# The low parts of split weights on one engine: a layer of attention and experts in fp32 on one core

## The chip, the cores and the metric

One core of a Trainium2 chip runs the whole layer in one launch. The metric is the device time of the execution in microseconds; before the change it is 1330.33 us, the median of 3 runs (1330.31 to 1330.54).

## The reference

256 latent tokens and 256 context tokens of width 1024 go through one layer. Cut to what matters:

```python
h, hc = modulate(x), modulate(ctx)                     # adaLN: RMS norm, scale and shift from c @ ada_w
q_a, k_a, v_a, qa_b, kva_b, gates = split(h @ w_in)    # the same for the context
o_a = attention(rope(norm(q_a)), [kc_a, k_a], [vc_a, v_a])        # 8 heads of 128, 2 of k and v
o_b = attention(mla_q(qa_b), mla_k(kva_b), mla_v(kva_b))          # 8 heads of 128 + 64
y = (sigmoid(g_a) * (o_a @ w_o_gqa) + sigmoid(g_b) * (o_b @ w_o_mla)) @ w_out
x = x + g1 * y
x = x + g2 * moe(modulate(x))                          # the best 4 of 32 experts for each token
```

Keys and queries are RMS-normed with a gain per channel. Of an expert's weights, w1 is 1024 x 2048 and w2 1024 x 1024, all fp32.

## The kernel before

**Two halves.** The first half, up to the choice of the experts, runs the layer's dense part. The second reads all 32 experts' weights, 12 parts of 1 MB each (`expert_part`, L99 to L106), through a ring of 20 buffers, and computes on 64 gathered tokens of each expert. 14 parts are loaded ahead of time by steps of the first half (`EZ` 2 parts, `EA` 8, `EG` 4), into buffers that attention has released; the other 6 buffers (three named w, y0, y1 and r0) come at its end. Each next part waits for a buffer that an expert has used up.

**Products in split precision.** The dense part multiplies in the format fp32r, and gets back the accuracy of fp32 by splitting each operand into a high part (a copy that is rounded) and a low part (what the rounding took off). `mm3` (L171) issues three matmuls: high by high (L173), high by low (L174), low by high (L175). Activations are split by `split` (L167), the copy on ScalarE and the subtraction on VectorE. Weights are split by `wsplit` (L132): the copy wh on ScalarE (L138) and the subtraction wl (L140) on VectorE for every fourth call and on GpSimd for the others. `wsplit` is called 124 times: 16 times in the first projection (`g1_cols`), 8 times in each of 12 chunks of 512 columns (`chunk`, L487: 2 of q, 4 of the gates, 2 each of the two branches' projections and the output's), 8 times in `mla_q` and 4 in `mla_a`. A chunk loads 4 rows of blocks at a time into one of three w buffers, which is free again after the last wh and wl made from it, and splits two blocks ahead of the product.

**Other work on GpSimd.** The rotary tables (`tables`, L397 to L425), the low part of V (L485), the gain of MLA's queries (L670), and in `mla_a` half of the scaling of the keys by their norms: L712 scales tokens' tiles 0 and 1 on GpSimd, L713 tiles 2 and 3 on VectorE, L714 the rotary part on VectorE. The norms come from a chain of some ten small VectorE instructions, `rsqrt` (L177 to L188).

**The order of the work.** Every piece of the first half is a Python generator, a work, which issues its instructions up to the next `yield` when a step of it is asked for. `PLAN` (L23) is a list of such steps, written out; `x*3` is three steps of x. Before a work's first step all works that it needs are finished (`step`, `finish` and `needs`), so the list is not the whole order: in both lists, for example, heads' scores are finished by the first step that needs them. Each engine, and SP as the queue of all loads, runs what it gets in its order; the compiler settles that order within the steps' neighbourhood, and the trace shows small instructions of different steps side by side.

The names that matter here: T0 and T1 transpose and norm the tokens; r, c, f, h, l, k 0 to 7 are the first projection; `bi` loads the experts' biases (3 loads); `tab` the rotary tables; `end` (`g1_end`) copies the projection's results; `ss` (`low_norms`) makes the norms; `kv` keys and values; q0, q1 and g0 to g3 the chunks of queries and gates; `mp`, p, a, b 0 to 3 prepare MLA's heads; S, P, V 0 to 15 are scores, transposed probabilities and values of the 16 heads; wa, wb, o the branches' and output's chunks; `rest` and `late` the last 12 and 4 units of the adaLN projection, each a load of 1 MB; x reloads the tokens; EZ, EA, EG load experts ahead.

```python
        self.nsplit += 1
        self.nc.scalar.copy(h, src)
        eng = self.nc.vector if self.nsplit % 4 == 0 else self.nc.gpsimd
        eng.tensor_sub(l, src, h.bitcast(F32))
```

Of the kernel before, what the change touches and what calls it, by code (L numbers as in the profile page):

```python
# [6 lines left out]
F32 = mybir.dt.float32  # L7
# [14 lines left out]
NA, NC, NS = 8, 4, 4  # L22
AHEAD = 2  # L23
PLAN = """
T0 bi l0 f1 h0 T0 h1 T0 f0 l1 k0 f2 r1 T1 h2 r0 k1 r2 T0 r3 T0 f3 k2 c2 h3 f4 k3 T0 T1 h4 T1 l4 T0 tab T1*2 r5
f5 f6 l3 k4 r4 r7 EZ c0 k5 c1 h6 l2 f7 k6 l5 end T1 q0 ss kv q0 h7 c3 q0 kv r6 q0 kv q1 kv q0*2 h5 q1*3 l7 q1
g0 q0 q1 q0*2 q1 kv EZ mp q1 q0 T1 g0 q1 q0 c7 k7 c5 g0*2 g1 q1*2 g0*3 g1 c4 g0 mp g0 g1 l6 EZ S0 g1*2 S2 g1*2
P0 kv rest g1 g2*3 mp S4 g2 P1 S2 S0 g2*2 end g3 rest*3 g2 rest g1 rest g3 V3 S1 g2 P2 rest P4 S4 V2 S3 c6 P3
g2 g3*3 S5 g3*2 a0 g3 rest S6 rest S1 a0 S5 rest a0 S6 g3 rest*2 a0 rest*3 P5 a0 rest*3 S3 g2 a0 S7 P6 g3 S7
rest V1 V6 a1 V0 rest a1 P7 b0 rest a1*2 S8 rest*2 a1 b0 rest V8 b1 V7 rest b1 rest a2 P9 b0 V5 b0 a1 b0 a0  # L30
rest a2 a1 V4 a2*2 S10*2 V9 b1 S8 a2 a3 a0 b0 V11 a3*4 rest a1 b2 wa0 S12 a3 a0 S9 P11 a2 wa0*2 a2 wa0 P8 wa0
rest wa0 S12 a2 b1 rest wa0*2 rest b1 b2 a3 b2 a1 rest wa0 rest P10 S9 S11 S13 b3 b2 wa1*3 a2 wa1 P12 a3 S13
wa1*3 S11 b3 V12 P13 b1 wa0 a3 b3 S14 V13 S14 EA S15 wb0 wa1 EA*2 wb0 wa1 wb0*2 EA wb0*2 b2 S15 wa1 wb0*3 b2
P14 EA wb1*2 b3 o0 wb1 EG o0 wb0 wb1 V10 rest*2 wb0 o0 P15 wb1 late wb1 o0 EA o0 wb1 o0*2 wb1 rest o0 EA wb1
o1 wb1 late EG*2 rest late o0 o1 o0*2 o1*5 V14 EG wb1 EG V15 wb0 late o1 o0 o1 late x b3 o1 wb1 late EA*2 o1
b3 late o1 late
"""
SLOTS = ("e0", "e1", "e2", "e3", "m0", "m1", "g0", "g1", "y0", "y1", "z0", "z1")
LATER = ("n0", "n1", "n2", "n3")
# [11 lines left out]
class Layer:  # L51
# [81 lines left out]
    def wsplit(self, src):  # L133

        shape = list(src.shape)
        h, l = self.tile("ws", shape, F32R, "wh", NS), self.tile("ws", shape, F32R, "wl", NS)
        self.nsplit += 1
        self.nc.scalar.copy(h, src)  # L138
        eng = self.nc.vector if self.nsplit % 4 == 0 else self.nc.gpsimd
        eng.tensor_sub(l, src, h.bitcast(F32))  # L140
        return h, l

    def bank(self, tag, shape=(128, 512), dt=F32):
# [539 lines left out]
    def mla_a(self, g):  # L683

        nc = self.nc
        G = self.grp[g]
        u = self.w([128, 512])
        nc.sync.dma_start(u, self.I["wmk"][g])
        kh, kl = self.wsplit(u)
        yield  # L690
        ssq, rs = G.pop("ssq"), self.m([128, 12], "grs")
        v = G["v"] = self.s(("e0", "x", "e1", "e0")[g], [128, 2, 4, 2, 128], F32R)
        kn = G["kn"] = self.h("k4", [128, 4, 2, 128])
        for t in range(4):
            ts = slice(t * 128, (t + 1) * 128)
            b = self.bank("acc")
            self.mm3(b, self.ckT[0][:, ts], self.ckT[1][:, ts], kh, kl, start=True, stop=True)
            bv = b.rearrange("p (h c d) -> p h c d", h=2, c=2)
            nc.scalar.copy(kn[:, t], bv[:, :, 0])
            sv = self.a([128, 2, 128])  # L700
            nc.scalar.activation(sv, kn[:, t], AF.Square)
            nc.vector.tensor_reduce(ssq[:, 4 + 2 * t:6 + 2 * t], sv, AX.X, OP.add)
            nc.scalar.copy(v[:, 0, t], bv[:, :, 1])
            nc.vector.tensor_sub(v[:, 1, t], bv[:, :, 1], v[:, 0, t].bitcast(F32))
            yield
        s4 = ssq[:, 4:12].rearrange("p (t h) -> p t h", h=2)
        nc.vector.tensor_add(s4, s4, self.ssr.unsqueeze(2).broadcast_to([128, 4, 2]))
        self.rsqrt(rs, ssq, 1.0 / 192, 12, "r12")
        nc.vector.tensor_scalar_mul(rs[:, 0:4], rs[:, 0:4], 192.0 ** -0.5)
        rk = rs[:, 4:12].rearrange("p (t h) -> p t h", h=2).unsqueeze(3)  # L710
        kr = self.a([128, 4, 2, 64])
        nc.gpsimd.tensor_mul(kn[:, 0:2], kn[:, 0:2], rk[:, 0:2].broadcast_to([128, 2, 2, 128]))  # L712
        nc.vector.tensor_mul(kn[:, 2:4], kn[:, 2:4], rk[:, 2:4].broadcast_to([128, 2, 2, 128]))  # L713
        nc.vector.tensor_mul(kr, self.rk.unsqueeze(2).broadcast_to([128, 4, 2, 64]), rk.broadcast_to([128, 4, 2, 64]))  # L714
        G.update(kr=kr, rs=rs)
        yield
# [572 lines left out]
```

## Time and profile before

| | |
|---|---|
| median of 3 runs | 1330.33 us (1330.31 to 1330.54) |
| the profiled execution | 1328.88 us |
| its span, first to last instruction | 1327.1 us |
| mean granted TensorE clock | 0.979 |
| TensorE busy (PE) | 1216.7 us, 92% |
| VectorE busy (DVE) | 445.8 us, 34% |
| ScalarE busy (ACT) | 289.1 us, 22% |
| GpSimd busy (POOL) | 158.9 us, 12% |
| read from HBM | 465.23 MB, 351 GB/s over the span |

PE, DVE, ACT and POOL are the names of the engines in the profile; SPq is the queue that issues the loads. A group is a line of the kernel, an engine, an operation and the tiles that it writes and reads; behind the bar come its busy time, the mean of one in ns, the idle time of the engine before it and what ended that. The shares of busy time are means over the whole span, of which the first half is less than a third.

### The profile page before, as it was taken

The numbers are of one execution on the slowest core, as the hardware profiler recorded it, in microseconds if no ns is written. First come the engines' busy times: TensorE is split into PE (matmuls) and PEld (weight loads), VectorE is DVE, ScalarE is ACT, GpSimd is POOL, SyncE is SP. The second block draws the span as 40 slices with busy tenths as digits, with TensorE's granted clock in tenths as the row PEclk, the third lists the DMA queues.
The fourth block names the chain that finished last, engine by engine and source line by source line (L and its number), as shares of the span: only waits on it lengthen the run. The fifth ranks groups of instructions, "written<-read, shape, count | busy, mean of one in ns | idle before, by whom it ended". The sixth has DMA issues, their size and how long they took to land.

```text
span 1327.1 us, 15523 instructions
## 1 busy us (share of the span) xinstructions
PE 1216.7 (92%) x6143; PEld 593.4 (45%) x6143; DVE 445.8 (34%) x940; ACT 289.1 (22%) x624; POOL 158.9 (12%) x181
## 2 busy tenths in 40 slices
PE   5989999799989989999999999999898998989896
PEld 4767766578752434333344333433333233333332
DVE  4468467875331332121221212212111122212112
ACT  2366667765420100000010000100000010000000
POOL 1566322343400000000000000000000000000000
PEclk8999999999989999999999999999999999999999
DMA  9825554147869999999999999999999999999995
GB/s 341 320 74 180 189 200 146 64 162 302 348 261 421 420 400 401 421 419 420 419 420 420 420 419 419 420 419 420 420 420 419 420 419 420 420 419 421 419 420 206
DMA packets 67325, 467.34 MB, mean 352 GB/s; under 512 B 7633, under 2 KB 8017, under 8 KB 11953
## 3 DMA queue, kind: packets, MB, share of 16 engines
q1 hardware_dynamic: 67248, 466.30, 86.7%
q8 instruction: 50, 0.82, 0.2%
q14 instruction: 27, 0.21, 0.0%
HBM read 465.23 MB, written 1.05 MB: 351 GB/s over the span
## 4 chain that ended last, share of the span: by engine, by line
PE 52%; DMA 34%; DVE 7%; ACT 2%; issue 2%; POOL 1%; SPq 0%; DVEq 0%; ACTq 0%; POOLq 0%
PE bs L1021 17%; PE bx L1055 10%; DMA r<-in_w_dram 8%; DMA m<-in_w_dram 8%; DMA n<-in_w_dram 7%; DMA w<-in_w_dram 6%; DMA e<-in_w_dram 4%; PE bacc L173 3%; PE bacc L174 3%; PE bacc L175 3%; PE bacc L989 2%; PE bx L191 2%; PE bt L989 2%; PE bacc L1070 1%; PE bs L1014 1%
## 5 line engine op out<-in xcount | busy, mean ns | idle before, releaser
L1030 ACT ACTIVATE a<-a 128x512 f32<-128x512 f32 x32 | 20.1, 630 | 728.9 <-DVE a L1029 728.9
L1029 DVE TENSOR_SCALAR a<-bs 128x512 f32<-128x512 f32 x32 | 22.1, 692 | 436.4 <-PE bs L1021 436.4
L140 POOL TENSOR_TENSOR wl<-w,wh 128x512 fp32r<-128x512 f32 (+1 forms) x81 | 105.8, 1318 | 145.6 <-ACT wh L138 128.7
L999 POOL TENSOR_TENSOR c<-c,gm 128x128 f32<-128x128 f32 x32 | 12.1, 399 | 867.8 <-DVE c L982 850.5
L1061 DVE TENSOR_TENSOR y<-bx,g 64x512 f32<-64x512 f32 x64 | 44.1, 688 | 211.7 <-PE bx L1055 211.0
L1021 PE MATMUL bs<-e,xg 128*64 128x512 f32 x416 | 94.2, 595 | 3.4 <-DMA e<-in_w_dram 3.4
L1021 PE MATMUL bs<-n,xg 128*64 128x512 f32 x400 | 90.8, 595 | 3.6 <-DMA n<-in_w_dram 3.5
L1021 PE MATMUL bs<-w,xg 128*64 128x512 f32 x312 | 72.2, 597 | 5.0 <-DMA w<-in_w_dram 5.0
L989 PE MATMUL bacc<-c,xn 128*128 128x128 f32 x256 | 40.8, 325 | 38.5 <-DVE c L982 37.8
L138 ACT CAST wh<-w 128x512 fp32r<-128x512 f32 (+1 forms) x108 | 65.0, 612 | 46.3 <-PE bacc L175 31.5
L989 PEld LDWEIGHTS bacc<-c,xn 128*128 128x128 f32 x256 | 37.3, 231 | 51.8 <-DVE c L982 51.0
L1021 PEld LDWEIGHTS bs<-e,xg 128*64 128x64 f32 x416 | 28.8, 137 | 66.5 <-issue 55.9
L1021 PEld LDWEIGHTS bs<-n,xg 128*64 128x64 f32 x400 | 27.7, 137 | 64.4 <-issue 56.5
L1021 PE MATMUL bs<-g,xg 128*64 128x512 f32 x208 | 47.7, 598 | 2.2 <-DMA g<-in_w_dram 2.2
L1021 PE MATMUL bs<-y,xg 128*64 128x512 f32 x208 | 47.4, 594 | 2.4 <-DMA y<-in_w_dram 2.4
L1055 PE MATMUL bx<-n,a 128*64 128x512 f32 x208 | 48.9, 614 | 0.7 <-ACT a L1043 0.7
L1021 PE MATMUL bs<-z,xg 128*64 128x512 f32 x208 | 47.5, 596 | 1.1 <-DMA z<-in_w_dram 1.1
L1055 PE MATMUL bx<-e,a 128*64 128x512 f32 x208 | 47.1, 595 | 0.0
L1021 PE MATMUL bs<-m,xg 128*64 128x512 f32 x192 | 44.2, 595 | 2.3 <-DMA m<-in_w_dram 2.3
L1021 PEld LDWEIGHTS bs<-w,xg 128*64 128x64 f32 x312 | 21.1, 136 | 54.0 <-issue 40.5
L989 PE MATMUL bt<-c,xn 128*128 128x128 f32 x256 | 37.3, 294 | 0.0
L989 PEld LDWEIGHTS bt<-c,xn 128*128 128x128 f32 x256 | 35.1, 212 | 0.0
(362 smaller groups left out, 2001.9 us busy)
## 6 DMA issues: line engine op xcount, KB each, us to landing
e<-in_w_dram SPq DMA_DIRECT2D x78, 1024.0 KB, 19.9
n<-in_w_dram SPq DMA_DIRECT2D x76, 1024.0 KB, 19.9
w<-in_w_dram SPq DMA_DIRECT2D x57, 1024.0 KB, 19.9
z<-in_w_dram SPq DMA_DIRECT2D x40, 1024.0 KB, 19.9
m<-in_w_dram SPq DMA_DIRECT2D x38, 1024.0 KB, 19.9
g<-in_w_dram SPq DMA_DIRECT2D x38, 1024.0 KB, 19.9
y<-in_w_dram SPq DMA_DIRECT2D x38, 1024.0 KB, 19.9
w<-in_ada_dram SPq DMA_DIRECT2D x24, 1024.0 KB, 6.5
```

The lines of the kernel that those rows point to most:

```text
L138: self.nc.scalar.copy(h, src)
L140: eng.tensor_sub(l, src, h.bitcast(F32))
L173: mm(o, lh, rh, start=start, stop=False, **kw)
L174: mm(o, lh, rl, start=False, stop=False, **kw)
L175: mm(o, ll, rh, start=False, stop=stop, **kw)
L191: self.nc.tensor.transpose(o, i, self.ident)
L989: nc.tensor.matmul(b[:, kk % 2], self.xn[:, t, kk * 128:(kk + 1) * 128], oh[:, t], start=t == 0, stop=t == 1)
L1021: mm(b[64 * j:64 * j + 64], xg[:, k, e % 2], w[:, lo:lo + 512], start=False, stop=k == 7, tile_position=(0, 64 * j))
L1029: v.tensor_scalar_min(g, gl, 7.0)
L1030: nc.scalar.activation(s, g, AF.Sigmoid, scale=1.702)
L1055: nc.tensor.matmul(b[64 * j:64 * j + 64], lh, w[:, i, j * 512:(j + 1) * 512], start=f == 0, stop=f == 7, tile_position=(0, 64 * j))
L1061: nc.vector.tensor_mul(y[r:r + 64, cs], b[q], self.g2[q, cs])
```

## The change

All 124 low parts of split weights are made on VectorE, and L712's half of the key scaling too, so that one engine makes L712 and L713 one after the other. `PLAN` is another list with the same works.

```diff
@@ PLAN @@
-T0 bi l0 f1 h0 T0 h1 T0 f0 l1 k0 f2 r1 T1 h2 r0 k1 r2 T0 r3 T0 f3 k2 c2 h3 f4 k3 T0 T1 h4 T1 l4 T0 tab T1*2 r5
-f5 f6 l3 k4 r4 r7 EZ c0 k5 c1 h6 l2 f7 k6 l5 end T1 q0 ss kv q0 h7 c3 q0 kv r6 q0 kv q1 kv q0*2 h5 q1*3 l7 q1
-g0 q0 q1 q0*2 q1 kv EZ mp q1 q0 T1 g0 q1 q0 c7 k7 c5 g0*2 g1 q1*2 g0*3 g1 c4 g0 mp g0 g1 l6 EZ S0 g1*2 S2 g1*2
-P0 kv rest g1 g2*3 mp S4 g2 P1 S2 S0 g2*2 end g3 rest*3 g2 rest g1 rest g3 V3 S1 g2 P2 rest P4 S4 V2 S3 c6 P3
-g2 g3*3 S5 g3*2 a0 g3 rest S6 rest S1 a0 S5 rest a0 S6 g3 rest*2 a0 rest*3 P5 a0 rest*3 S3 g2 a0 S7 P6 g3 S7
-rest V1 V6 a1 V0 rest a1 P7 b0 rest a1*2 S8 rest*2 a1 b0 rest V8 b1 V7 rest b1 rest a2 P9 b0 V5 b0 a1 b0 a0
-rest a2 a1 V4 a2*2 S10*2 V9 b1 S8 a2 a3 a0 b0 V11 a3*4 rest a1 b2 wa0 S12 a3 a0 S9 P11 a2 wa0*2 a2 wa0 P8 wa0
-rest wa0 S12 a2 b1 rest wa0*2 rest b1 b2 a3 b2 a1 rest wa0 rest P10 S9 S11 S13 b3 b2 wa1*3 a2 wa1 P12 a3 S13
-wa1*3 S11 b3 V12 P13 b1 wa0 a3 b3 S14 V13 S14 EA S15 wb0 wa1 EA*2 wb0 wa1 wb0*2 EA wb0*2 b2 S15 wa1 wb0*3 b2
-P14 EA wb1*2 b3 o0 wb1 EG o0 wb0 wb1 V10 rest*2 wb0 o0 P15 wb1 late wb1 o0 EA o0 wb1 o0*2 wb1 rest o0 EA wb1
-o1 wb1 late EG*2 rest late o0 o1 o0*2 o1*5 V14 EG wb1 EG V15 wb0 late o1 o0 o1 late x b3 o1 wb1 late EA*2 o1
-b3 late o1 late
+f0 h0 f1 T0 bi T0 h1 T0 l0 l1 k0 f2 r1 T1 k1 r2 r0 c2 r3 T0*2 f3 k2 h3 f4 k3 T0 T1*2 h4 T1 T0 tab T1 r5 f5 f6
+l3 h2 l4 k4 r4 r7 c0 EZ k5 c1 f7 k6 l2 h6 end T1 q0*4 q1 kv*2 ss q0 kv r6 q0 q1 kv q1*2 h5 l7 q1 q0 q1*2 g0 q0
+kv q0 EZ mp rest*2 q1*2 q0 T1 g0 q0 g0 c7 g0 g1 c5 g0 c3 q1 g1 q1 g0*3 mp g1*2 g2 kv h7 S0 g2 EZ l6 P0 g0 g1*2
+rest g2 g1*2 S2 mp P1 g2*3 g3 rest g2 g3 rest g1 rest S1 c4 S2 P2 l5 end g2 S0 rest S4 S6 rest V3 V2 S4 S3 P3
+g3 rest g3*2 S5 S3 c6 g3*2 g2 P4 a0 g3 rest*2 a0 S6 g3 a0 rest a0*2 P5 rest*2 S5 rest V1 rest g2 S7 P6 rest*3
+g3 S7 V6 a1 rest b0 k7 rest V0 a1*3 P7 S8 rest*2 a1 rest a0 V8 rest b1 V7 b1 b0 S1 b0 rest a2 P9 b0 V5 a0*2
+rest a2 a1 a2*2 a1 b0 S10*2 V9 V4 a2 a3 b1 rest wa0 b0 b2 S8 V11 a3*4 a1 P13 a1 wa0 a3 a2*2 wa0 S12 rest*2 wa0
+S12 rest b1 wa0 P8 wa0 b1 rest wa0 b2 P12 S11 S13 wa0 wa1 rest S9 S15 a3 P10 b2 wa1 wa0 a2 wa1 S9 a2 a3 S13
+wa1*3 b3 a0 wa1 S11 b3 V12 V13 b2 S14*2 EA a3 wa1 wb0 b3 EA wb0 b2 P11 wb0 EA S15 wa1 wb0*3 rest wb0 EA wa1
+wa0 wb1 b3 wb0*2 wb1 P14 b2 EA wb1 o0 late o0 wb1 rest wb1 o0 P15 wb1 late wb1 EA o0 wb1 o0*2 b1 o0 EA wb1
+o1*2 wb1 late o0 o1*2 o0 EG*2 o1 o0*2 rest o1 V14 EG*2 V15 wb0 wb1 late wb0 o0 wb0 o1 late x EG V10 rest o1 b3
+o1 EA wb1 late*3 EA b3 o1*3
@@ wsplit @@
-        eng = self.nc.vector if self.nsplit % 4 == 0 else self.nc.gpsimd
-        eng.tensor_sub(l, src, h.bitcast(F32))
+        self.nc.vector.tensor_sub(l, src, h.bitcast(F32))
@@ mla_a @@
-        nc.gpsimd.tensor_mul(kn[:, 0:2], kn[:, 0:2], rk[:, 0:2].broadcast_to([128, 2, 2, 128]))
+        nc.vector.tensor_mul(kn[:, 0:2], kn[:, 0:2], rk[:, 0:2].broadcast_to([128, 2, 2, 128]))
```

With what each first step finishes written out, the lists differ in these places. `r0`, `c0` come ahead of T0, and T1 ahead of the second unit of the projection; `bi` comes behind that unit. The second half of `end`, and `ss`, came after one step of q0 and now come after four of q0 and one of q1. Two steps of `rest` stand in the midst of q1. wa0 begins ahead of the last scores of heads 10 and 11 and not behind their values, and the scores of 12 and 13 stand together ahead of most of wa0. EA's last three loads and EG's first, which came right behind o0's first step, now stand behind its third, seventh and ninth; EG's other three move by a step or two. `late` begins behind o0's first step and ends ahead of o1's last three, where its last step was the last of all.

## Rows read from the trace of the kernel before

**Rows 1.** Busy time by stage (a:b, us, then PE, PEld, DVE, ACT, POOL, PEclk, DMA, GB/s).

```profile
30.00:70.00 40.00, 39.69 (x275) 30.32 (x274) 20.43 (x44) 14.01 (x32) 18.97 (x35) 1.00 0.80 307
70.00:98.00 28.00, 22.91 (x95) 17.46 (x94) 17.46 (x32) 18.66 (x53) 19.36 (x21) 0.94 0.21 75
98.00:190.00 92.00, 89.45 (x507) 68.81 (x509) 57.67 (x136) 63.74 (x127) 39.46 (x31) 1.00 0.49 169
190.00:270.00 80.00, 68.18 (x450) 49.11 (x442) 66.07 (x180) 56.37 (x135) 19.13 (x18) 0.96 0.36 129
270.00:376.00 106.00, 105.16 (x578) 81.11 (x576) 54.07 (x106) 54.91 (x111) 45.42 (x34) 1.00 0.72 276
376.00:390.00 14.00, 9.79 (x60) 8.07 (x61) 8.25 (x39) 5.86 (x12) 0.76 (x2) 0.76 0.78 317
390.00:1327.10 937.10, 865.74 (x4106) 326.54 (x4104) 208.47 (x359) 67.63 (x141) 11.35 (x30) 0.98 0.99 409
```

**Rows 2.** The same view, two microseconds at the first expert.

```profile
390.00:392.00 2.00, 2.00 (x10) 0.62 (x10) 0.00 (x0) 0.16 (x1) 0.00 (x0) 1.00 0.00 0
```

**Rows 3.** Timeline of SP, the issue of loads, 376 to 393 us.

```profile
376.80 0.74 SPq L105 DMA_DIRECT2D r<-in_w_dram  x1
391.83 0.33 SPq L105 DMA_DIRECT2D z<-in_w_dram  x1
```

**Rows 4.** The chain that ended last, 0 to 390 us, by line.

```profile
by line: PE bacc L173 9.1%; PE bacc L174 8.7%; PE bacc L175 8.5%; issue 4.3%; PE bx L278 4.3%; DMA w<-in_ada_dram 3.6%; PE bt L191 3.2%; POOL wl L140 2.6%; PE bx L191 2.5%; PE bt L174 2.2%; PE bt L175 2.1%; PE bt L173 2.0%; PE bs L173 2.0%;
```

**Rows 5.** Line 140, the low parts: ns min/median/max, first and last start; who waited.

```profile
L140 POOL TENSOR_TENSOR wl<-w,wh x81: 1012/1303/1759, 70.8 to 365.6; 128x512 fp32r<-128x512 f32 x75, 128x384 fp32r<-128x384 f32 x6
...
L140 DVE TENSOR_TENSOR wl<-w,wh x27: 548/693/2007, 78.0 to 366.3; 128x512 fp32r<-128x512 f32 x25, 128x384 fp32r<-128x384 f32 x2
...
  PE bt L174: 3.4, 4
```

**Rows 6.** Timeline of POOL and of DVE, 83 to 89 us (start, us).

```profile
83.41 4.22 POOL L140 TENSOR_TENSOR wl<-w,wh 128x512 fp32r<-128x512 f32 x3
...
83.92 1.23 DVE L182 TENSOR_SCALAR r_v<-kssq 128x14 f32<-128x14 f32 x1
86.44 1.23 DVE L186 TENSOR_TENSOR r_t<-krstd 128x14 f32<-128x14 f32 x1
88.11 0.17 DVE L186 TENSOR_TENSOR r_t<-krstd 128x14 f32<-128x14 f32 x1
```

**Rows 7.** Timeline of POOL and of SP, 44 to 52 us.

```profile
44.59 0.21 POOL L405 COPY rb<-h 128x32 f32<-128x32 f32 x1 [5.36 <-DMA h<-in_rows_dram]
50.04 1.29 POOL L140 TENSOR_TENSOR wl<-h,wh 128x512 fp32r<-128x512 f32 x1
...
51.36 0.33 SPq L321 DMA_DIRECT2D h<-in_wg_dram  x1
```

**Rows 8.** Busy time by stretch, around the first rsqrt chain.

```profile
84.00:94.00 10.00, 5.22 (x19) 3.38 (x20) 8.54 (x19) 4.45 (x13) 5.82 (x6) 1.00 0.00 0
94.00:97.40 3.40, 3.40 (x10) 2.66 (x9) 1.53 (x4) 1.80 (x5) 3.00 (x6) 0.52 0.83 308
```

**Rows 9.** Line 140 alone by stage: DVE busy, POOL busy, PEclk, DMA, GB/s.

```profile
98.00:190.00 92.00, 8.13 (x9) 37.87 (x29) 1.00 0.49 169
190.00:270.00 80.00, 2.52 (x3) 10.51 (x9) 0.96 0.36 129
270.00:376.00 106.00, 10.62 (x12) 43.91 (x33) 1.00 0.72 276
```

**Rows 10.** Groups of instructions, 190 to 270 us: the scaling of MLA's keys.

```profile
L713 DVE TENSOR_TENSOR k<-k,grs 128x512 f32<-128x512 f32 x3 | 4.0, 1333 | 0.0
L712 POOL TENSOR_TENSOR k<-k,grs 128x512 f32<-128x512 f32 x3 | 3.6, 1209 | 18.0 <-DVE grs L188 18.0
L714 DVE TENSOR_TENSOR a<-rk,grs 128x512 f32<-128x512 f32 x3 | 3.2, 1051 | 0.0
```

**Rows 11.** PE's waits, 0 to 390 us (in total, times, longest).

```profile
PE bx L278 <- DMA w<-in_ada_dram: 3.6, 3, 1.4
```

## The prediction

> **What bounds the kernel now.** The span of the core is 1327.1 us. The profiled execution took 1328.88 us, 1.45 below the median of the three runs, 1330.33; the sum below is made against the first and carried to the second by the same difference. I cut the span into stages [rows 1]. From 390 us on the DMA engines are busy 99% of the time and move 409 GB/s: the experts' weights arrive no faster than that, and 409 GB/s over 937.1 us is 383 MB, the 364 parts of 1.049 MB that are still to come (384 less the 20 that lie in SBUF by then) and the output. The change touches nothing there.
>
> What starts this stream is the first expert matmul. Between 390 and 392 us the DMA engines stand still [rows 2]: the last of the 20 buffers was issued at 376.80, and the next load, at 391.83, could only be issued when the first expert had used up z0 [rows 3]. So the time is the moment at which the experts begin, plus a constant: a microsecond won or lost before 390 us is won or lost at the end, as long as the 20 parts are there in time. For that there is room: 28% of 270 to 376 and 22% of 376 to 390 us, 30 + 3 = 33 us of idle DMA [rows 1].
>
> Ahead of 390 us the reader is to look at what PE lacks in each stage [rows 1]: 0.3 us of 40 in 30 to 70, 5.1 of 28 in 70 to 98, 2.6 of 92 in 98 to 190, 11.8 of 80 in 190 to 270, 0.8 of 106 after it. A gain has to come out of these, or out of time at the lower clock. The chain of waits up to 390 us is mostly PE; POOL's low parts hold 2.6% of it, 10.1 us [rows 4].
>
> **What the change removes.** Of the 124 low parts every fourth is made on VectorE now, so 93 are POOL's, at a median of 1.30 us; VectorE takes 0.69 [rows 5]. PE waited 3.4 us, in 4 cases, for POOL's low parts on their largest line [rows 5], and the view names no wait for one of VectorE's. Two more things are less plain:
> - POOL holds VectorE up. While POOL made three low parts in a row from 83.41 on, an r_v and an r_t of 14 elements took 1.23 us each on VectorE; with POOL done, at 88.11, the same line took 0.17 [rows 6]. A VectorE low part takes 2.0 us at most where the median is 0.69 [rows 5]: one POOL low part fits into the difference. This goes with POOL's instructions. The Trainium skill ("SBUF — State Buffer", "Who interferes with whom") calls it an exclusive lock of the port pair that the two engines share, for a whole instruction; the trace agrees, 2.0 being 0.69 + 1.30. By it the 1.23 fall to 0.17; without it they would stay, and 2 of the 5 us that I take below at 84 us would drop out.
> - POOL's low parts stand in a queue with its other work. The rotary tables began at 44.59, after POOL had waited 5.36 us for a load, and low parts stood between them; the weight load of 51.36 waited for the one that began at 50.04 [rows 7].
>
> **Stage by stage, the terms of the sum.**
> - 30 to 70 us: the low parts leave the queue behind the tables, so that load can go up to 5 us earlier. PE lacks only 0.3 us here [rows 1]. Between 0 and 5, I take 1, near PE's row. The three loads of `biases`, now behind the second pair of weight loads, are needed by no one before the experts: nothing.
> - 70 to 98 us: PE works 5.22 us of the 10 from 84 on, waiting for POOL's low parts and for ScalarE, which waited for the rsqrt chain that POOL had stretched; then it runs 3.4 us at 0.52 of its clock, the 1.2 GHz level, which costs 0.48 of them, 1.6 us [rows 8]. The change takes both causes away and, beside that, puts the second half of `g1_end` and `low_norms` behind three more steps of q0 and the first of q1, so that PE has those products to do meanwhile. What these two issue on ACT and DVE moves past the copies and low parts of that stretch, and the load of q1's first unit goes ahead of it on SP. Between 0 and 6.4, I take 5. The low part of V (L485) stays on POOL and can still hold VectorE up once.
> - 98 to 190 us: 29 low parts move [rows 9]. If they were late as often as POOL's were in that row (4 of 93) by one instruction of VectorE, this would cost 29 × 4 / 93 × 0.69 = 0.9; the most to be had is PE's 2.6. I take 1.
> - 190 to 270 us, the MLA heads: VectorE is busy 66 of 80 us and POOL makes 9 low parts and 3 key scalings there [rows 1, 9, 10]. Twelve instructions more at 0.69 are 8.3 us. Against that, L713 takes 1333 ns and L714 1051 where 690 would do, 3 × (0.64 + 0.36) = 3.0 us, and the same holds for the small instructions that I can't count. The key scaling itself: L712 takes 1209 ns beside L713's 1333; after the change the two follow each other, 2 × 0.69 = 1.38, so that pair costs nothing. The bounds are a loss of 8.3, all twelve in the way, and a gain of 11.8, all that PE lacks. I take a gain of 2, close to the middle: VectorE's own load hardly grows, and each low part is there 0.6 us sooner.
> - 270 to 376 us: 33 low parts [rows 9], PE lacks 0.8 [rows 1]; as above a loss of 33 × 4 / 93 × 0.69 = 1.0 or a gain of 0.8. I take 0.5.
> - The moved steps. Of `rest`, two steps go ahead of most of g0 and the others are spread more evenly; each unit is a load of 1 MB, its products and a copy or an addition. PE waited 3.6 us in all for these loads [rows 11], so 3.6 either way; I take 0. `late` (4 such loads) now begins right behind o0's first step and ends before o1's last three, on the same PE, with the same work: 0. wa0's first load and splits go ahead of the last of heads 10 and 11, five low parts' time (3.5 us) at most, in a stretch counted above. EA's last three expert loads and EG's first go behind up to eight steps of o0, on SP's queue past the loads of wout and `late`. This would cost only beyond the 33 us of idle DMA above, so nothing; with that cover gone each part is 2.6 us (1.049 MB at 409 GB/s).
>
> The sum: 1 + 5 + 1 + 2 + 0.5 = 9.5 us less, 1319.4 in a profiled execution and **1320.8** as a median.
>
> **Rivals.**
> - VectorE becomes the bound in the MLA stretch (slower). In-order, a low part now stands behind a reduction that waits for scores, and a rsqrt chain behind low parts. Price: the 8.3 in full, 0.9 and 1.0 in the neighbouring stages, less the 5 at 84 us, which doesn't hang on it: 5.2 later, 1335.5. For it: 66 of 80 us busy already. Against it: part of those 66 are POOL's doing. It decides from some 74 of the 80 us on (66 + 8.3, no relief).
> - Nothing that can be told (within 0.2%, 2.7 us, which is about what a measurement of this kernel can tell from no change). PE waited just 3.4 us for low parts; where they come sooner, the next wait takes over, a load of the ada weights or ScalarE's copies, which stand ahead of every low part and don't change. It would give 1329. The Trainium skill ("Perfetto Trace Analysis", "Optimizing Scalar/DVE Operations") warns that offloading between VectorE and GpSimd might not help, because they share a read port; by that rule the time stays where it is. The rows speak half against it: port time falls from 1.30 to 0.69 per low part.
> - Far more: the chain's 10.1 us of POOL halve, the stretch from 84 us closes (6.4), and half of what PE lacks from 190 to 270 us goes (6): 17 us, 1313. Against it: VectorE's 8.3 us have to go somewhere.
>
> **How the numbers follow.** The forecast, 3 to 14 us faster, has 0.58; far more, 0.12; no change, 0.12; VectorE as the bound, 0.18. So faster 0.70, same 0.12, slower 0.18. The range leaves out the far half of the last case and the far half of "far more": 1311 to 1335. Its upper end is also about the sum of the lower bounds (0 + 0 - 0.9 - 8.3 - 1.0, with the 5 at 84 us). The likeliest case's own range is 1316 to 1328.
>
> **What would show it.** Right: the experts begin near 380 us, with the DMA engines idle just before; PE is busy over 8 of the 10 us around the first rsqrt chain, and the clock doesn't fall there; r_t never takes over 0.3 us from then on save beside V's split; L713 near 0.69. VectorE's low parts: 124 at a median near 0.69. Wrong: PE waits for VectorE's low parts for more than the 3.4 us that it now waits for POOL's; VectorE busy over 74 of the 80 us of the MLA stretch; PE's idle time there above 11.8; or no idle DMA before the first expert load that follows a free buffer, which would mean that the 20 parts came late.

## The result and the profile after

The changed kernel takes **1318.58 us** (median of 4 runs, 1318.11 to 1319.53), the kernel before 1330.42 beside it (4 runs, 1330.31 to 1330.54): a ratio of 0.9912, with an interval of 0.9895 to 0.9929, 11.8 us less. The prediction was 1320.8 us, faster. Lines behind the edit in the function that splits weights are one lower than before: its low part is L139 now, the key scaling L711 to L713.

The profiled execution took 1318.76 us, its span is 1317.0. From the page, the busy time of the engines:

```profile
PE 1220.3 (93%) x6143; PEld 594.7 (45%) x6143; DVE 475.4 (36%) x1037; ACT 289.3 (22%) x624; POOL 36.8 (3%) x84
```

GpSimd lost 122 us of work and VectorE won 30. Busy time by stage comes next (a:b, us, then PE, PEld, DVE, ACT, POOL, PEclk, DMA, GB/s); the stages are those of [rows 1], the bounds at 376 and 390 us moved to where the same work ends now and the others kept, so that the work between them is not quite the same, and behind them the first rsqrt chain, the two microseconds behind the first expert matmul, and all that lies ahead of it:

```profile
30.00:70.00 40.00, 40.00 (x275) 30.79 (x274) 20.39 (x51) 14.41 (x32) 9.38 (x26) 1.00 0.77 301
70.00:98.00 28.00, 26.13 (x130) 20.25 (x129) 22.92 (x49) 23.17 (x62) 7.36 (x11) 1.00 0.41 151
98.00:190.00 92.00, 91.02 (x534) 67.39 (x534) 69.48 (x177) 62.60 (x128) 1.67 (x2) 1.00 0.50 182
190.00:270.00 80.00, 73.80 (x434) 54.29 (x434) 70.63 (x209) 61.66 (x147) 5.31 (x6) 0.98 0.35 127
270.00:362.70 92.70, 90.94 (x499) 70.84 (x497) 58.50 (x104) 44.73 (x87) 0.00 (x0) 1.00 0.73 277
362.70:376.70 14.00, 10.69 (x74) 8.24 (x74) 7.92 (x38) 4.93 (x12) 0.76 (x2) 0.76 0.90 345
376.70:1317.00 940.30, 868.89 (x4110) 329.05 (x4106) 208.69 (x359) 68.83 (x141) 11.39 (x30) 0.98 0.99 408
78.00:88.00 10.00, 9.24 (x39) 6.96 (x38) 9.24 (x24) 8.13 (x28) 2.19 (x2) 1.00 0.30 116
...
376.70:378.70 2.00, 2.00 (x14) 0.77 (x12) 0.00 (x0) 0.00 (x0) 0.00 (x0) 1.00 0.01 4
0.00:376.70 376.70, 351.37 (x2038) 265.66 (x2038) 266.69 (x678) 220.47 (x483) 25.45 (x54) 0.97 0.60 223
```

The same view of the kernel before, up to its first expert matmul:

```profile
0.00:389.85 389.85, 350.80 (x2038) 266.71 (x2038) 237.29 (x581) 221.35 (x484) 147.55 (x151) 0.97 0.58 215
```

Read the two last rows against each other. PE does the same 2038 matmuls in the same 351 us, but in a span 13.15 us shorter: all of the gain is time that PE stood idle (39.05 us before, 25.33 after). VectorE has 97 instructions more (93 low parts and 4 scalings). At the 0.60 us from one to the next that the timeline below shows, they would add 58 us. They add 29.4. The other 29 us are time by which VectorE's other instructions had been longer: those that the edit doesn't touch, group by group the same number in both traces, take 24.7 us less in sum, and the low parts that were VectorE's already another 6.

That shows in line 139 itself (ns min/median/max, first and last start), the row that answers to [rows 5]:

```profile
L139 DVE TENSOR_TENSOR wl<-w,wh x108: 537/692/2467, 68.9 to 352.7; 128x512 fp32r<-128x512 f32 x100, 128x384 fp32r<-128x384 f32 x8
```

and in the timeline of VectorE around the first rsqrt chain, which answers to [rows 6]:

```profile
77.84 3.67 DVE L139 TENSOR_TENSOR wl<-w,wh 128x512 fp32r<-128x512 f32 x3 [0.37 <-ACT wh L138]
81.44 0.16 DVE L181 TENSOR_SCALAR r_v<-kssq 128x14 f32<-128x14 f32 x1
...
81.84 0.17 DVE L185 TENSOR_TENSOR r_t<-krstd 128x14 f32<-128x14 f32 x1
...
83.45 0.68 DVE L139 TENSOR_TENSOR wl<-w,wh 128x512 fp32r<-128x512 f32 x1
84.05 0.16 DVE L185 TENSOR_TENSOR r_t<-krstd 128x14 f32<-128x14 f32 x1
```

r_v and r_t take 0.16 and 0.17 us, where they took 1.23 each. The median of the low parts stayed (693 to 692 ns), but one of them takes 2.47 us: it is one of the three from 77.84 on (3.67 together), and the timeline of GpSimd says beside what it ran:

```profile
77.37 2.39 POOL L484 TENSOR_TENSOR m<-y,m 128x1024 fp32r<-128x1024 f32 x1 [1.54 <-ACT m L483]
```

That is the low part of V, the one large subtraction which stayed on GpSimd.

In the stretch from 190 to 270 us the key scaling, as groups (busy us, mean ns), for [rows 10]:

```profile
L711 DVE TENSOR_TENSOR k<-k,grs 128x512 f32<-128x512 f32 x4 | 2.7, 684 | 0.0
L712 DVE TENSOR_TENSOR k<-k,grs 128x512 f32<-128x512 f32 x4 | 2.7, 680 | 0.0
L713 DVE TENSOR_TENSOR a<-rk,grs 128x512 f32<-128x512 f32 x3 | 2.0, 682 | 0.0
```

PE's waits up to 376.7 us (in total, times, longest), for [rows 5, 11]:

```profile
PE bx L277 <- DMA w<-in_ada_dram: 2.5, 2, 1.4
...
PE bt L173 <- DVE wl L139: 0.8, 1, 0.8
```

and the queue of loads at the start of the experts, for [rows 3]:

```profile
366.27 0.44 SPq L105 DMA_DIRECT2D r<-in_w_dram  x1
378.68 0.33 SPq L105 DMA_DIRECT2D z<-in_w_dram  x1
```

**Where the time went.** Following the same piece of work in both timelines: the copy that ends the first projection starts 1.3 us earlier (74.76 to 73.48), the first scaling of a key behind the rsqrt 4.7 (89.37 to 84.67), the last tanh of the gates 6.7 (181.20 to 174.52), the last scaling of MLA's keys (the half that moved) 11.9 (279.33 to 267.45), the last step of the output's second chunk 13.7 (373.17 to 359.44), and the first expert matmul 13.15 (389.85 to 376.70). But the span is only 10.1 us shorter: 3.05 us are given back behind the first expert matmul (937.25 us to the end before, 940.30 after). These are single executions. In a second trace of the new kernel the first expert matmul is at 378.03 and the end 940.57 behind it. The kernel before has one trace, and one of a kernel that differs from it only behind this matmul has the first scaling of a key at 91.25 and the last tanh at 183.37, some 2 us later. So a stage's gain is known to a microsecond or two.

### The profile page after: what moved, and what is told of

The parts are those of the page before. It is cut to its first block, busy times and chain, and to the rows that moved or that the text cites. A ratio compares the mean times of both kernels' runs of the same rounds, so it can differ in the third digit from the quotient of the medians.

```text
span 1317.0 us, 15464 instructions
## 1 busy us (share of the span) xinstructions
PE 1220.3 (93%) x6143; PEld 594.7 (45%) x6143; DVE 475.4 (36%) x1037; ACT 289.3 (22%) x624; POOL 36.8 (3%) x84
## 4 chain that ended last, share of the span: by engine, by line
PE 65%; DMA 27%; DVE 5%; ACT 2%; issue 1%; SPq 0%; POOL 0%; DVEq 0%; ACTq 0%; POOLq 0%
PE bs L1020 21%; PE bx L1054 11%; DMA r<-in_w_dram 8%; DMA m<-in_w_dram 6%; DMA n<-in_w_dram 5%; DMA e<-in_w_dram 5%; PE bacc L172 3%; PE bacc L173 3%; PE bacc L174 3%; DMA w<-in_w_dram 3%; PE bacc L988 2%; PE bx L277 2%; PE bx L190 2%; PE bacc L1069 2%; PE bt L988 2%; PE bt L1069 2%
## 5 line engine op out<-in xcount | busy, mean ns | idle before, releaser
L139 DVE TENSOR_TENSOR wl<-w,wh 128x512 fp32r<-128x512 f32 (+1 forms) x108 | 74.6, 696 | 30.1 <-ACT wh L138 29.4
```

The lines of the kernel that those rows point to most:

```text
L139: self.nc.vector.tensor_sub(l, src, h.bitcast(F32))
```

## The experiments

The theory: GpSimd's low parts read SBUF, and while they do, VectorE's instructions stand still; taking them away frees VectorE, whose results PE waits for. A first rival says that the new order of the work does it, and the engines nothing. A second says that it is GpSimd's queue, and that a low part is simply there 0.6 us sooner. A question of its own is where the 3 us went.

### The engines and the order apart

One kernel has the new engines in the order of before, the other the old engines in the new order: `PLAN` of one file stands in the other.

> Only the engines change: all low parts and the key scaling on VectorE, the list of steps is that of before. Theory A (the gain comes from POOL's work leaving: shorter low parts, and VectorE no longer held up): at least two thirds of the 11.8 us, so 1318 to 1322.5 us. Rival B (the gain comes from the new order): 1326 or more. Rival C (VectorE in the old order is in the way, and the new list was needed to avoid that): 1331 or more.

> Only the list of steps changes, three of four low parts and half of the key scaling stay on POOL. Theory A: a gain of at most 4 us, 1326 to 1331. Rival B: 1322 or less. If the two parts add up, this one's gain is 11.8 less that of the engines alone; if they don't, each needs the other.

Measured: the engines alone 1322.36 us (9 runs), a ratio of 0.9944 (0.9928 to 0.9961); the order alone 1330.6 us (10 runs), 1.0006 (0.9989 to 1.0023). So the engines give 7.4 us, a little under the two thirds of 11.8 that theory A asked for (7.9), though inside its range of times; the order by itself gives nothing that can be told, and the two together 11.8: the order is worth some 4 us once the engines are changed (the intervals of 0.9944 and 0.9912 just touch), and only then. In the profiles the first expert matmul is at 382.17 and 388.53, against 376.70 with both. The first r_v takes 0.16 us with the engines alone and 1.27 with the order alone: what held it up goes with the engines. The first scaling of a key starts at 88.70 and 88.38 us, against 89.37 before and 84.67 with both: most of what the order adds is there by then.

### GpSimd reads again

```diff
         self.nc.vector.tensor_sub(l, src, h.bitcast(F32))
+        if self.nsplit % 4:
+            for j in range(0, 256, 64):
+                d = self.tile("ws", [128, 64], F32, "du", 1)
+                self.nc.gpsimd.tensor_sub(d, h.bitcast(F32)[:, j:j + 64], h.bitcast(F32)[:, j:j + 64])
```

> The changed kernel, and beside each low part that POOL made before, POOL subtracts 4 times 64 columns of wh from themselves into a tile that nobody reads: POOL is as busy as before, but nobody waits for it. If POOL's reading holds VectorE up and that cost the time: 3 us or more slower than the changed kernel, 1321.5 to 1326, with small VectorE instructions beside POOL's again longer than alone. If only the length of the low parts and POOL's queue mattered: within 1 us of the changed kernel, 1317.6 to 1319.6.

Measured: 1327.16 us (10 runs), 0.9986 (0.9972 to 1.0). The gain is nearly gone, a little more of it than was expected, but this doesn't settle by what. The added instructions read the high part, so they also keep its buffer: ScalarE waits 17.5 us in all, 15 times, for GpSimd before it can write the next one. And they are short, so that VectorE's small instructions beside them take 0.26 to 0.31 us at most. Either could be the cause, so three more were made in which GpSimd holds neither a high nor a low part; it still reads a few columns of each loaded unit.

### GpSimd reads what nobody waits for

```diff
+                d, b = self.tile("ws", [128, 64], F32, "du", 1), self.b12[64:128, 0:512]
+                nc.gpsimd.tensor_copy(d, units[kk // 4][:, 0, 0:64])
+                for _ in range(3):
+                    nc.gpsimd.tensor_sub(b, b, self.zero[64:128].broadcast_to([64, 512]))
```

It stands in the loop of a chunk, once for each load of w; the subtractions of zero are made in place, on the experts' biases. The unchanged new kernel ran again beside it.

> The changed kernel itself, as the measure for the three beside it on the same chip. From the first comparison (0.9912): about 11.7 us under the kernel before.

> The changed kernel, and for each of the 24 units of four weight blocks that the 12 chunks load, POOL reads 64 columns of the unit and then three times subtracts zeros from the experts' first biases, 512 columns, in place: as long as three low parts, read from SBUF, and no buffer that anyone waits for is held by it (the look before this one held wh, and ScalarE waited 17.5 us for that). If POOL's reading holds VectorE up and that cost time: 2 to 6 us slower than the changed kernel, and low parts on VectorE of up to 2 us again. Rival (only the low parts' own length, or the queue on POOL, mattered): within 1 us of it.

Measured: the new kernel 1319.06 us (6 runs), 0.9912 (0.9895 to 0.993), as the first time. With the reads 1356.79 us, 1.0202 (1.018 to 1.0224): far more than any theory gave, and the trace shows why it can't be used. Nothing tied the subtractions to the loads, so the 72 of them (1173 ns in the mean) ran in two long rows from 23.63 us on, 34 ahead of the tables and 36 ahead of V's low part on GpSimd's queue; that part came at 124.42 us in place of 77.37. Only one line of it is of use: the first 12 low parts, most of which had those reads beside them, have a median of 1252 ns (653 without).

The next tied them down: each group of three subtracts a zero that GpSimd makes from one column of the load.

```diff
+                d, b = self.tile("ws", [128, 1], F32, "du", 2), self.b12[64:128, 0:512]
+                nc.gpsimd.tensor_scalar_mul(d, units[kk // 4][:, 0, 0:1], 0.0)
+                for _ in range(3):
+                    nc.gpsimd.tensor_sub(b, b, d[64:128].broadcast_to([64, 512]))
```

> The look with POOL's long reads once more: there POOL did all 72 subtractions in a row from the start, ahead of the rotary tables and V's low part, because nothing tied them to their units, and 37 us went. Here each subtraction takes off a zero that POOL has made from the unit's first column, so the three come when the unit has landed. If POOL's reading holds VectorE up and that cost time: 2 to 6 us slower than the changed kernel (1321 to 1325 beside its 1319.06), with low parts on VectorE of up to 1.9 us. Rival (only the low parts' own length, or the queue on POOL, mattered): within 1 us of it.

Measured: 1346.83 us (5 runs), 1.0126 (1.0103 to 1.0149), 27.8 us over the new kernel: over what was expected, by a lot. Its timelines of VectorE and of GpSimd around the first rsqrt chain:

```profile
83.10 2.41 POOL L484 TENSOR_TENSOR m<-y,m 128x1024 fp32r<-128x1024 f32 x1 [1.53 <-ACT m L483]
...
86.81 3.64 POOL L498 TENSOR_TENSOR b<-b,du 64x512 f32<-64x512 f32 x3
...
87.19 1.01 DVE L181 TENSOR_SCALAR r_v<-kssq 128x14 f32<-128x14 f32 x1
88.23 0.18 DVE L183 TENSOR_SCALAR krstd<-r_v 128x14 int32<-128x14 int32 x1
88.44 0.90 DVE L185 TENSOR_TENSOR r_t<-krstd 128x14 f32<-128x14 f32 x1
89.37 0.17 DVE L186 TENSOR_TENSOR r_t<-r_t,r_v 128x14 f32<-128x14 f32 x1
89.46 1.54 DVE L139 TENSOR_TENSOR wl<-w,wh 128x512 fp32r<-128x512 f32 x1
90.92 0.16 DVE L187 SCALAR_TENSOR_TENSOR krstd<-r_t,krstd 128x14 f32<-128x14 f32 x1
91.12 0.17 DVE L185 TENSOR_TENSOR r_t<-krstd 128x14 f32<-128x14 f32 x1
```

In the 3.64 us of GpSimd's three subtractions, which touch nothing of VectorE's, three of VectorE's instructions are held up, each by 0.7 to 0.9 us, and the ends of r_v and r_t, 88.20 and 89.34, are 1.14 us apart, about the length of one of GpSimd's subtractions (3.64 / 3 = 1.2); when these are over, r_t's line is back at 0.17. So the picture of [rows 6] returns with other reading work on GpSimd. And it costs VectorE in sum what the change had won:

```profile
0.00:400.00 400.00, 358.15 (x2013) 269.15 (x2014) 297.19 (x674) 220.12 (x481) 121.11 (x150) 0.95 0.56 206
```

VectorE's 674 instructions take 297.19 us, where 678 took 266.69 in the new kernel: 30.5 us more with no work added to it, about the 29 us that the change had given back. The 27.8 us at the end are not all due to it: GpSimd's queue is fuller too, and PE waits 3.5 us in all for the gain of MLA's queries, which GpSimd makes, where it waited 1.2.

### GpSimd busy, but reading next to nothing

The same place; in place of three subtractions, 18 times a constant written into a tile that nobody reads. The one read of 64 columns of each unit stays.

```diff
+                for _ in range(3):
+                    for _ in range(6):
+                        nc.gpsimd.memset(d, 0.0)
```

> The same as the look with long reads, but POOL writes zeros 18 times to 64 columns instead, and reads nothing but the first 64 columns of each unit. If it is the reading that holds VectorE's instructions with two inputs: within 1 us of the changed kernel. If any work of POOL's does (or the one read of each unit, which holds the weight's buffer): as slow as with the long reads.

Measured: 1318.34 us (6 runs), 0.9908 (0.9892 to 0.9925), no other than the new kernel beside it. The group, and its busy time by stretch:

```profile
L499 POOL MEMSET du<- 128x64 f32 x432 | 65.7, 152 | 24.6
...
0.00:380.00 380.00, 356.13 (x2047) 267.15 (x2049) 266.62 (x678) 220.40 (x483) 96.62 (x510) 0.99 0.59 221
```

GpSimd is busy 71 us longer than in the new kernel (96.62 to 25.45), nearly six tenths of the 122 that it lost by the change, and VectorE's 678 instructions still take 266.6 us. A busy GpSimd, and a fuller queue of it, cost nothing here; its reading does. The Trainium skill ("SBUF — State Buffer", "Who interferes with whom") says this of two-input instructions: they contend with a GpSimd instruction that reads SBUF, and not with one that only writes it. The two kernels agree with that.

What is not shown is how the 7.4 us of the engines divide between VectorE being freed and the moved low parts being there sooner (1.30 us against 0.69): no run has the one without the other. PE's waits that name GpSimd's low parts were 3.8 us in the kernel before.

### How much room VectorE had

```diff
         self.nc.vector.tensor_sub(l, src, h.bitcast(F32))
+        self.nc.vector.tensor_sub(l, src, h.bitcast(F32))
```

> The changed kernel with each of the 124 low parts made twice in a row on VectorE: 0.6 us more of VectorE for each, 74 us in all, 7.2 of them in 190 to 270 us where VectorE is busy 70.6 of 80. If VectorE has room (low parts are two blocks ahead of PE): under 4 us slower than the changed kernel. If VectorE in its order sets the pace by now: 10 us or more.

Measured: 1351.02 us (5 runs), 1.0157 (1.0134 to 1.018), 32 us over the new kernel for 124 × 0.60 = 74 us of instructions more on VectorE, whose busy time up to the first expert matmul grows by 65.7 us (266.69 to 332.43): between 0.43 and 0.49 of each microsecond that VectorE gets reaches the end. Its busy time in the two stages with the most splitting and norms:

```profile
98.00:190.00 92.00, 82.89 (x449) 60.91 (x449) 81.20 (x188) 57.59 (x118) 7.96 (x6) 0.98 0.44 153
190.00:270.00 80.00, 68.89 (x450) 48.57 (x449) 72.65 (x212) 57.01 (x137) 6.52 (x8) 1.00 0.42 148
```

PE lacks 9 of the 92 and 11 of the 80 us there, where it lacks 1 and 6 in the new kernel. VectorE need not be busy all the time to set the pace: it runs what it gets in its order, and in this kernel 72.65 of 80 us was enough.

### The key scaling alone

```diff
-        nc.vector.tensor_mul(kn[:, 0:2], kn[:, 0:2], rk[:, 0:2].broadcast_to([128, 2, 2, 128]))
+        nc.gpsimd.tensor_mul(kn[:, 0:2], kn[:, 0:2], rk[:, 0:2].broadcast_to([128, 2, 2, 128]))
```

> The changed kernel with L712's half of the key scaling on POOL as before, four instructions. If the pair costs the same either way (2 times 0.69 in a row, or 1.2 beside 1.3): within 1 us of the changed kernel. If VectorE was relieved by it in the MLA stretch: up to 2 us faster; if POOL's instruction on the path to the transposes is what cost: up to 3 us slower.

Measured: 1319.23 us (6 runs), 0.9912 (0.9892 to 0.9932): moving this half is worth nothing that can be told. Groups of this kernel:

```profile
L711 POOL TENSOR_TENSOR k<-k,grs 128x512 f32<-128x512 f32 x4 | 6.1, 1514 | 72.2 <-DVE grs L187 22.6 <-ACT a L577 19.4 <-ACT a L575 17.1
...
L712 DVE TENSOR_TENSOR k<-k,grs 128x512 f32<-128x512 f32 x4 | 2.7, 684 | 0.0
```

Here VectorE's half is not held up at all, and GpSimd's takes 1.51 us. In the timeline the first pair begins at 192.72 on VectorE and at 192.83 on GpSimd.

### The 3 us given back

Beside the third expert (e == 2) the sum of the output biases is made: 4 small products into two banks in turn, so that the third has to wait until VectorE has read the first (it begins at 456.12 us, VectorE's reading ends at 456.07). Windows of the new kernel there, 79 us behind the first expert matmul:

```profile
456.00:460.00 4.00, 4.00 (x7) 1.29 (x8) 3.56 (x7) 0.00 (x0) 0.00 (x0) 0.53 1.02 424
460.00:464.00 4.00, 4.00 (x12) 1.06 (x12) 1.26 (x2) 0.00 (x0) 0.00 (x0) 0.62 0.40 164
464.00:468.00 4.00, 4.00 (x22) 1.26 (x18) 0.00 (x0) 0.00 (x0) 0.00 (x0) 1.00 0.91 311
```

The granted clock falls to 0.53, the 1.2 GHz level, in the stretch in which VectorE works on the sum; the expert's own matmuls that follow start at that clock, and 16 of them take 5.26 us from 459.77, the next 16 3.60. SP issues no load for 13.9 us, until 463.36, and DMA falls to 0.40. What the queue waits for between 440 and 470 us (in total, times, longest) is PE, which has yet to use the full buffers up:

```profile
SPq L105 <- PE bx L1054: 17.8, 4, 13.9
SPq L105 <- PE bs L1020: 7.9, 6, 1.3
```

From 520 us on DMA is at 1.01 in every window of 20 us and moves 418 to 421 GB/s, until the loads end: there a short pause of PE should cost nothing. The kernel before does the same: 80 to 90 us behind its first expert matmul the clock is 0.84 and DMA 0.91. Its clock falls later, from 469.6 us on, when the sum's matmuls are all but done, where in the new kernel the last four of eight run at the lower clock; and SP's longest wait for PE is 12.7 us in place of 13.9.

```profile
469.80:479.80 10.00, 10.00 (x43) 2.94 (x44) 3.40 (x6) 0.00 (x0) 0.00 (x0) 0.84 0.91 356
```

The edit that follows moves the sum 14 experts on, into that later stretch. It was made on the new kernel, on the kernel before, and on the new kernel with V's low part on VectorE as well:

```diff
-            if e == 2:
+            if e == 16:
```

> The changed kernel with the experts' output bias added beside expert 16 and not beside expert 2. The experts begin 13.1 us earlier after the change, and the end comes 10.1 earlier; the trace has idle DMA engines (0.40 busy from 460 to 464 us) just where TensorE runs at 0.53 to 0.62 of its clock beside that addition. If this is where 3 us went: 1314.5 to 1316.5, with no idle DMA between 400 and 520 us. If the difference has another cause, or PE only pays the same later: 1318 to 1319.5.

> The kernel before with the output bias beside expert 16. If the addition beside expert 2 costs the kernel before as much as the changed one: 3 us under the kernel before. If the change made that place worse (the profiled spans from the first expert matmul to the end are 937.3 us before, 940.3 after, 935.5 with the bias later): 1.5 to 2 us under it.

> The changed kernel with the output bias beside expert 16, and V's low part (1024 columns, 2.39 us on POOL, which held a low part of VectorE's for 2.43 us) on VectorE too. Theory: bias later gives 2 to 3 us (1315.55 beside the first runs' 1318.6), V's low part 0.5 to 1.5 more: 3 to 4.5 us under the changed kernel. Rival: VectorE pays for V's low part itself ahead of the first rsqrt chain (1.2 us) and nothing is won by it: 2 to 3 us under the changed kernel.

Measured: 1315.55 us on the new kernel (4 runs), 0.9896 (0.9866 to 0.9926), as expected; 1324.76 on the kernel before (8 runs), 0.9956 (0.9941 to 0.997), 5.9 us and more than either case expected, where the first expert matmul is at 389.69 against 389.85, so that all of it is won behind it; and with V's low part **1313.64** (5 runs), 0.9876 (0.9858 to 0.9895), the fastest of all, 5.4 us under the new kernel beside it, where 3 to 4.5 were expected. The windows of that last kernel, 80 to 90 us behind its first expert matmul, and its low parts:

```profile
455.70:465.70 10.00, 10.00 (x52) 3.01 (x50) 1.38 (x2) 0.00 (x0) 0.00 (x0) 1.00 1.02 422
...
L139 DVE TENSOR_TENSOR wl<-w,wh x108: 537/691/742, 70.3 to 352.0; 128x512 fp32r<-128x512 f32 x100, 128x384 fp32r<-128x384 f32 x8
```

The clock no longer falls there and DMA doesn't stop: the sum of the biases is what cost time at this place. At its new place the clock falls too (0.71 in 840 to 850 us of the last kernel), but DMA stays at 1.01. From the first expert matmul to the end it is 935.5 and 935.7 us with the sum later, 940.3 in the new kernel.

But the sum explains only part of the 3.05 us, since it cost the kernel before as well: there the same stretch falls from 937.25 to 933.5. With the sum later in both, the new kernel is still 2.0 us longer behind its first expert matmul, and what these are isn't shown. Nor do the medians say that the sum costs the new kernel more: moving it gains the kernel before 5.9 us and the new one 3.5 or less. On the new kernel alone the gain is not told apart from none (the intervals of 0.9896 and 0.9912 overlap); on the kernel before it is, and on the third kernel that of the two edits together is. The longest low part is 742 ns now, so V's part was the last thing that held one up. What V's part is worth by itself isn't known: no kernel had that edit alone.

## Why the prediction was right

The sign, the mechanism and nearly the size: 9.5 us were forecast, 11.8 measured. That the size came so near is in part luck: ahead of the experts 13.15 us were won in the trace, 3.65 more than the sum said, and behind them 3.05 were lost that it didn't foresee. By its own steps:

- **What bounds the kernel.** That the start of the experts is what counts, with the 20 parts in time, held: the DMA engines are idle again behind the first expert matmul (0.01 in 376.70 to 378.70), and the next load waits for z0. "Plus a constant" was wrong by 3.05 us. The prediction read [rows 1] for the stage behind 390 us as one mean, 99% DMA, and said that the change touches nothing there. It did not look into it: 79 us in, beside the sum of the biases, the loads wait for PE and the stream stops, some 1.2 us longer in the new kernel than before. Some 2 us of the 3.05 lie elsewhere, and their cause stays open. It isn't the engines or the order alone: from the first expert matmul to the end the two kernels that have only one of them take 935.2 and 936.7 us.
- **VectorE held up by GpSimd.** This was the reason for the terms at 84 us and in the MLA stretch, and it is the one that the runs bear out best: 58 us of added work cost VectorE 29.4, reads on GpSimd bring the 0.9 and 1.0 us and 30.5 us of VectorE's time back, writes don't.
- **30 to 70 us**, taken as 1: 1.3.
- **70 to 98 us**, taken as 5: 3.4 (the gain grows from 1.3 to 4.7 by the first scaling of a key). The clock stays at 1.00, as foreseen, and PE is busy 9.24 of 10 us where it had 5.22 [rows 8]. V's low part held VectorE up once, as was said, by 1.8 us (2.47 less 0.69), at the head of this chain. The step had counted on the order too, on products of q0 and q1 to fill the wait, and rightly: with the engines alone the gain up to this mark is 0.7 us (the first scaling of a key is at 88.70, against 89.37 before and 84.67 with both).
- **98 to 190 us**, taken as 1, the most to be had 2.6: 2.0.
- **190 to 270 us, the MLA heads**, taken as 2, between -8.3 and 11.8: this is the term that was mis-sized. The gain goes from 6.7 (last tanh of the gates) to 11.9 (last scaling of MLA's keys): 5.2 us. The step took a value close to the middle since "VectorE's own load hardly grows". It grows from 66.07 to 70.63 us of 80, about half of the 8.3, and stays under the 74 of the rival, while PE's lack falls from 11.8 to 6.2. With the old order the engines alone gain 3.3 us between the same two marks (2.9 to 6.2), so most of this is the engines'.
- **270 to 376 us**, taken as 0.5: 1.3 (11.9 to 13.15).
- **The moved steps**, taken as 0: right for the order alone (1.0006). With the new engines the order is worth some 4 us, but most of it shows at the first rsqrt chain, where the prediction had counted it, under 70 to 98 us. What it didn't say is that this part of the order is worth little with the old engines (1.0 us at that mark, nothing at the end). No load of the ada weights came later by it: PE waited 2.5 us for them in place of 3.6.
- **The key scaling pair**, "costs nothing": it is worth nothing either (0.9912 with and without).

Of the rivals, VectorE as the bound did not come about (PE waits 0.8 us for its low parts at one group, where it waited 3.4 for GpSimd's), but its mechanism is real and near: made twice, each added low part costs 0.26 us at the end (32 / 124). "Nothing that can be told" rested on the next wait taking over; that wait, for the ada weights, fell from 3.6 to 2.5 us instead. Up to the experts the 13.15 us lie about halfway between the forecast's 9.5 and the 17 of "far more". The Trainium skill warns that offloading between VectorE and GpSimd might not help ("Perfetto Trace Analysis", "Optimizing Scalar/DVE Operations"). Moving the work from GpSimd to VectorE did help in this kernel, where the engines alone give 0.9944.

## What to carry to other kernels

Where VectorE is loaded and GpSimd does elementwise work on SBUF beside it, look for VectorE's shortest instructions and for the longest of a common kind: if they are long by one GpSimd instruction, moving the work to VectorE may cost it much less than its nominal time, here 29 of 58 us. An order of work that is worth nothing with one assignment of engines can be worth a third of the gain with another, so the two are tried together. And a stage that is called a constant is cut into pieces of a few microseconds before it is believed: a small piece of dependent work (four biases' sums) placed where the loads wait for PE cost the two kernels some 2 to 6 us.

## What had not been expected of the hardware

In the cases looked at, the engine that begins later pays. In the kernel before, r_v on VectorE, begun 0.51 us behind a low part of GpSimd's, was held to 1.23 us [rows 6]; with the scaling back on GpSimd, begun 0.05 to 0.11 us behind VectorE's, GpSimd's takes 1.48 to 1.53 us in all four cases and VectorE's 0.68. The kernel before has it both ways in its key scaling: at 200.09 and 279.30 us VectorE begins 0.03 us ahead and takes 0.68 to GpSimd's 1.55; at 232.07 GpSimd begins 0.03 us ahead and takes 1.04 to VectorE's 1.55. So the order of two instructions of the same work can put the wait on the engine that has the time for it.

VectorE's instructions with one input tile (r_v, a TENSOR_SCALAR of 128x14 elements) were held up just as those with two: 1.23 us in the kernel before, 1.01 with GpSimd's reads put back, 0.16 without.
